# A decoder trunk's first stage: norm gains packed with the first tile of x, key weights in tiles of their own, first transfers in another order, first squares on Pool

## The chip, the cores and the metric

The kernel runs on one core of one Trainium2 chip. The core has TensorE (PE in the rows; PEld is its weight load), VectorE (DVE), ScalarE (ACT), GpSimd (POOL) and SyncE (SP), which here issues every transfer. They run side by side, each in the order of its own instructions, and wait for each other by semaphores. The metric is the device time of one execution in microseconds (us), the median of several runs.

## What is computed

Two layers of a decoder trunk over 576 tokens: 512 of a prompt and 64 of eight decode streams (8 tokens each, with 256 tokens in a paged cache). The model width is 1024.

```python
def decoder_layer(x, p_i, pos, ret_s0, past, topk, g_norm, w_in, q_gain, k_gain,
                  w_o_ret, w_o_att, w_out, w_ple_gate, w_ple_proj):
    h = rmsnorm(x, g_norm)
    rq, rk, rv, rz, aq, ak, av, az, iq, ik, iw, gr, ga = in_projection(h, w_in, pos, q_gain, k_gain)
    o_r, s_new = retention(rq, rk, rv, ret_s0)
...
    u_r = jnp.einsum('bte,ed->btd', o_r * jax.nn.silu(rz), w_o_ret)
...
    u_a = jnp.einsum('bte,ed->btd', o_a * jax.nn.silu(az), w_o_att)
    m = jax.nn.sigmoid(gr) * u_r + jax.nn.sigmoid(ga) * u_a
    x = x + jnp.einsum('btd,de->bte', m, w_out)
    gate = jax.nn.sigmoid(jnp.einsum('btd,de->bte', x, w_ple_gate))
    x = x + gate * jnp.einsum('btp,pd->btd', p_i, w_ple_proj)
    return x, ak, av, ik, s_new
```

Here `rmsnorm` divides x by the root of the mean of its squares over the 1024 channels and multiplies by a gain per channel, and `o_a` is an attention over keys that an indexer selects (top 128 of the prompt, top 66 of a decode stream). What the change touches is the norm of x and the projection to the indexer's key, the attention's key and its value (`ik`, `ak`, `av`: 64 + 128 + 128 = 320 columns).

## The kernel before

**Layout.** x lies with channels on the 128 partitions: eight tiles (k = 0 to 7) of 128 channels by 576 tokens. To keep precision, each operand of a product is split in a high part and a low rest, and a product is three matmuls: high by high, low by high, high by low. `put_x` makes them of a tile of x: ACT writes `xh` (x by the gain, rounded), DVE writes `xl` (x by the gain, less `xh`), and ACT copies the last 64 columns of `xl` behind `xh` (the "tail", used for the decode tokens). A weight tile `wst` becomes `whi` (ACT) and `wlo` (DVE, `wst` less `whi`) in `convert`.

**The norm's divisor** isn't applied to x. `put_x` also squares each tile of x (ACT, into `ssq`, shown as `rot`, or into slots of `misc`), and DVE adds the squares up tile by tile. When all eight are in, `stats` has PE sum over the channels (ten matmuls `tr<-ones,rot`), DVE and POOL make the reciprocal root `rcol`, and the results of the projections are scaled by it afterwards.

**The first stage** is `proj_kx`: for each k and each of five groups of tokens it multiplies `xh`, `xl` by the key weights of that k, into five banks (oT, acc, tq, pm, pm). That is 14 matmuls of 320 columns for each k, 112 in all; the last two k are done together, bank by bank. The key weights come in five parts (`KX_PARTS`: k 0, k 1, k 2 and 3, k 4 and 5, k 6 and 7), of 160 or 320 KB, through the same two `wst` and three `whi`/`wlo` slots as every other weight. Then the ten matmuls of `stats` follow, then the indexer's query projection (`iq`, 260 columns, weights in three parts), then the other projections. Layer 1 runs the same `proj_kx` at the end of layer 0.

**The order of the work** is made by the recorder `Streams` when the program is built: each generator yields operations, the recorder keeps a clock for every engine from its own table of durations, and takes next the operation that could start first (ties by priority). What it writes down is a fixed order on each engine; on the chip the semaphores alone decide when each starts. All operations are recorded in one helper, so that nearly all rows have its line, L309.

Of the kernel before, what the change touches and what calls it, by code (L numbers as in the profile page):

```python
# [21 lines left out]
KT = D // 128  # L22
NP = 512
NS = 64
T = NP + NS
TH = T // 2
TX = T + NS
DEPTH = 2
# [295 lines left out]
def tile_hybrid_decoder(ctx: ExitStack, tc: tile.TileContext, A, O):  # L324
    nc = tc.nc
    ctx.enter_context(tc.manual_schedule())
    K = Streams()
    V, S, PE, SP, G = (Engine(n, o) for n, o in (("DVE", nc.vector), ("ACT", nc.scalar), ("PE", nc.tensor),
                                                 ("SP", nc.sync), ("POOL", nc.gpsimd)))
# [36 lines left out]
    gn = cp.tile([128, DEPTH, KT], FT, name="gn")  # L366
# [5 lines left out]
    ssq = rot[:, 0:TX]  # L372
# [35 lines left out]
        K.set(paged)  # L408

    ready, paged = Event(), Event()  # L410
    second, third = Event(), Event()


    W = {}

    class Unit:
        def __init__(self, srcs):
            self.srcs, self.parts, self.ev = srcs, [], Event(len(srcs))
            self.evs = [Event() for _ in srcs]

    def plan(l):
        def b(key, n, per):
            src = A[key[0]][l] if len(key) == 1 else A[key[0]][l, key[1]]
            return [(src[:, k * n:min(KT, k + per) * n], (min(KT, k + per) - k) * n) for k in range(0, KT, per)]

        def a(i):
            return [(A["wa"][l, i], 1024)]

        for st in PLAN:
            name, i = st[0], st[1:]  # L430
            if name == "kx":
                srcs = [(A["wk"][l][:, a * 320:z * 320], (z - a) * 320) for a, z in KX_PARTS]
            elif name == "iq":
                srcs = b(("wq",), 260, 3)
            elif name in ("rv", "aq"):
                srcs = b(("wb", i[0] + (0 if name == "rv" else 2)), 256, 4)
            elif name in A_UNITS:
                srcs = a(A_UNITS[name] + i[0])
            elif name == "wo":
                srcs = [(A["wo"][l, i[0]], 1024)]  # L440
            elif name == "pp":
                srcs = [(A["wpp"][l, i[0]], 1024)]
            else:
                continue
            u = Unit(srcs)
            W[(l,) + st] = u
            yield u

    stage_ev = {}

    def load_weights(units):
        for n, (u, src, size) in enumerate(units):
            if n == 1:
                yield second
            if n == 3:
                K.set(third)
            t = yield Get(WST)
            yield SP.dma_start(t[:, :size], src)
            K.spawn(convert(u, t, size, stage_ev[n], stage_ev[n + 1]), PRIO["convert"])

    def convert(u, t, size, prev, done):
        yield prev
        hi = yield Get(WHI)
        lo = yield Get(WLO)
        yield S.activation(hi[:, :size], t[:, :size], AF.Copy)
        yield V.tensor_tensor(lo[:, :size], t[:, :size], hi[:, :size].bitcast(FT), OP.subtract)
        K.put(WST, t)
        K.set(u.evs[len(u.parts)])
        u.parts.append((hi, lo))
        K.set(u.ev)  # L470
        K.set(done)
# [48 lines left out]
    def proj_kx(u, xh, xl, evs):  # L520
        banks = []
        for name in ("oT", "acc", "tq", "pm", "pm"):
            banks.append((yield Get(BANK[name])))
        for i, (k0, k1) in enumerate(KX_PARTS):
            yield u.evs[i]
            if k1 < KT:
                order = [(k, j) for k in range(k0, k1) for j in range(5)]
            else:
                order = [(k, j) for j in range(5) for k in range(k0, k1)]
            for k, j in order:  # L530
                yield evs[k]
                hi, lo = (w[:, (k - k0) * 320:(k - k0 + 1) * 320] for w in u.parts[i])
                if j < 4:
                    c = slice(j * 128, (j + 1) * 128)
                    terms = ((xh[:, k, c], hi), (xl[:, k, c], hi), (xh[:, k, c], lo))
                else:
                    terms = ((xh[:, k, NP:TX], hi), (xh[:, k, NP:TX], lo))
                for n, (x, w) in enumerate(terms):
                    yield PE.matmul(banks[j][:, :320], x, w, start=k == 0 and n == 0,
                                    stop=k == KT - 1 and n == len(terms) - 1)  # L540
            K.put(WHI, u.parts[i][0])
            K.put(WLO, u.parts[i][1])
        return banks

    def split(hi, lo, x):
# [11 lines left out]
        yield G.tensor_tensor(dst, m[:n, :w], mh[:n, :w], OP.pow)  # L557
        K.put(RSM, m)

    def put_x(x, k, l, xh, xl, zs, first):  # L560
        yield S.activation(xh[:, k, :T], x, AF.Copy, scale=gn[:, l, k:k + 1])
        yield V.scalar_tensor_tensor(xl[:, k, :], x, gn[:, l, k:k + 1], xh[:, k, :T].bitcast(FT),
                                     op0=OP.mult, op1=OP.subtract)
        yield S.activation(xh[:, k, T:TX], xl[:, k, NP:T].bitcast(FT), AF.Copy)
        if k == 0:
            yield S.activation(ssq[:, :T], x, AF.Square)
            K.set(first)
        else:
            yield first
            sq = yield Get(zs)  # L570
            yield S.activation(sq, x, AF.Square)
            yield V.tensor_tensor(ssq[:, :T], ssq[:, :T], sq, OP.add)
            K.put(zs, sq)

# [3 lines left out]
    def layer(l, xh, xl, kxb):  # L578
# [818 lines left out]
        pl = lb.tile([128, 2, T], FR, name="pl")  # L1397
        pst = lb.tile([128, 2, T], FT, name="pst")

        def load_p():  # L1400
            yield SP.dma_start(pst, A["pT"][l])
            yield from split(ph, pl, pst)
# [76 lines left out]
        def ple2(d, th, ev):  # L1479
            yield ev  # L1480
            if last:
                K.put(ZS, th)
            else:
                yield e_pp[d]
                yield V.scalar_tensor_tensor(th, th, 1.0, pp[:, d], op0=OP.add, op1=OP.mult)
                yield V.scalar_tensor_tensor(xa[:, d], th, 0.5, xa[:, d], op0=OP.mult, op1=OP.add)
                K.put(ZS, th)
                yield from put_x(xa[:, d], d, l + 1, nh, nl, ZS, e_sq)
                K.set(e_n[d])
                yield SP.dma_start(xd[:, d, :], xa[:, d])  # L1490
            K.set(e_e)

        for d in range(KT):
# [11 lines left out]
    def main():  # L1505
        xh = xp.tile([128, KT, TX], FR, name="xh")
        xl = xp.tile([128, KT, T], FR, name="xl")
        K.spawn(setup(), 0)
        units = [(u, s, n) for l in range(DEPTH) for u in plan(l) for s, n in u.srcs]
        for n in range(len(units) + 1):  # L1510
            stage_ev[n] = Event(0 if n == 0 else 1)
        K.spawn(load_weights(units), PRIO["load"])
        evs = [Event() for _ in range(KT)]
        e_sq = Event()
        zs = zslots(0, 4)
        stc = tc.tile_pool(name="st", bufs=1, reuse_waits="tile")
        st = stc.__enter__()

        def load(k):
            x = st.tile([128, T], FT, name=f"x{k}")  # L1520
            if k > 3:
                yield third
            yield SP.dma_start(x, A["xT"][:, k, :])
            if k == 0:
                yield SP.dma_start(gn, A["norm_gain"])
                K.set(second)
            yield from put_x(x, k, 0, xh, xl, zs, e_sq)
            K.set(evs[k])

        for k in range(KT):  # L1530
            K.spawn(load(k), 2 if k else 0)
        K.spawn(setup2(), 3)
        kxb = yield from proj_kx(W[0, "kx"], xh, xl, evs)
        stc.__exit__(None, None, None)
        for l in range(DEPTH):
            xh, xl, kxb = yield from layer(l, xh, xl, kxb)
# [2 lines left out]
    K.go()  # L1539


KX_PARTS = ((0, 1), (1, 2), (2, 4), (4, 6), (6, 8))
BANKS = {"pm": 3, "tq": 1, "ta": 1, "oT": 1, "tr": 1, "acc": 1}
A_UNITS = {"az": 0, "rq": 4, "rk": 8, "rz": 12, "gr": 16, "ga": 24, "wout": 32, "wpg": 40}
# [19 lines left out]
def _prepare(x_prompt, x_sample, cache_k, cache_v, cache_idx_k, state_ret, page_table, p_prompt, p_sample,  # L1564
# [3 lines left out]
    def chan(a):  # L1568
        a = np.asarray(a)
        return a.reshape(a.shape[:-1] + (a.shape[-1] // 128, 128))  # L1570

    def tok(ap, as_):
        return np.concatenate([np.asarray(ap).reshape(NP, -1), np.asarray(as_).reshape(NS, -1)], 0)
# [1 line left out]
    d = {}  # L1575
    d["consts"], d["rot"] = _const_array()
    d["page_table"] = c(np.asarray(page_table).reshape(1, 16))
    d["norm_gain"] = c(chan(norm_gain).transpose(2, 0, 1))
    d["qk_gain"] = c(np.stack([np.asarray(q_norm_gain), np.asarray(k_norm_gain)], 1).reshape(-1))
    d["xT"] = c(chan(tok(x_prompt, x_sample)).transpose(2, 1, 0))  # L1580
    d["pT"] = c(np.stack([chan(tok(p_prompt[i], p_sample[i])).transpose(2, 1, 0) for i in range(DEPTH)]))
    w_in = np.asarray(w_in)
    offs = np.cumsum([0, 512, 512, 512, 512, 512, 128, 128, 512, 256, 64, 4, 1024, 1024])
# [60 lines left out]
```

## Time and profile before

| what | value |
|---|---|
| time, median of 3 runs | 1097.97 us (1097.46 to 1100.9) |
| the profiled execution's own time | 1100.1 us |
| its span, from the first to the last instruction | 1098.2 us |
| PE busy | 98% of the span |
| DVE busy | 69% |
| ACT busy | 48% |
| POOL busy | 6% |
| granted TensorE clock, mean | 0.997 |

The profile is of one execution. A busy PE need not be PE at its peak, since matmuls overlap; the time from one matmul's start to the next one's tells more. "Idle" before an instruction is the idle time of its engine, with what ended it.

### The profile page before, as it was taken

Reading aid. Unit: us, or ns where it says so; the run is one execution under the profiler, and the core shown is the slowest. Engines: PE = TensorE matmul, PEld = TensorE weight load, DVE = VectorE, ACT = ScalarE, POOL = GpSimd, SP = SyncE. Lnnn points to the kernel's source line nnn. Section 1 sums busy time; section 2 is a strip of 40 time slices with the busy share of each in tenths; the row PEclk is TensorE's granted clock in tenths of the full one; section 3 lists DMA queues with packets and bytes.
Section 4 is the critical chain, followed back from the end, with each engine's and each line's share of the span. In section 5 each row is a group of like instructions: output and inputs, shape, how many; then the busy total and the mean of one; then the engine's idle time right before and its main releaser. Section 6 shows DMA issues by size and latency. Waiting matters only on the chain.

```text
span 1098.2 us, 21521 instructions
## 1 busy us (share of the span) xinstructions
PE 1074.9 (98%) x8330; PEld 1048.6 (95%) x8330; DVE 759.6 (69%) x1963; ACT 527.4 (48%) x1112; POOL 68.6 (6%) x110
## 2 busy tenths in 40 slices
PE   7999999999999999999999999999999999999998
PEld 7989999989999999999999998999899999999998
DVE  6799999985455576543658999999854556655343
ACT  6743355676455442335446433656654555222421
POOL 0200012111000000000011001121101000000000
PEclk9999999999999999999999999999999999999999
DMA  6531222223333265533344322223232324554231
GB/s 204 162 118 69 88 80 96 76 83 110 113 103 108 103 198 158 184 93 104 99 124 133 108 71 74 81 99 106 91 121 91 121 90 144 184 184 136 82 115 49
DMA packets 53112, 124.85 MB, mean 114 GB/s; under 512 B 7443, under 2 KB 19603, under 8 KB 53011
## 3 DMA queue, kind: packets, MB, share of 16 engines
q1 hardware_dynamic: 53010, 123.49, 34.7%
q8 instruction: 65, 1.06, 0.4%
q14 instruction: 37, 0.30, 0.1%
HBM read 103.12 MB, written 20.35 MB: 112 GB/s over the span
## 4 chain that ended last, share of the span: by engine, by line
PE 68%; DVE 24%; issue 3%; DMA 1%; ACT 1%; SPq 1%; POOL 0%; DVEq 0%; POOLq 0%; ACTq 0%
PE pm L309 57%; DVE xl L309 6%; DVE sm L309 4%; DVE wlo L309 3%; PE tq L309 3%; PE oT L309 3%; DVE misc L309 2%; PE ta L309 2%; PE acc L309 2%; DVE silz L309 2%; PE tr L309 1%; DVE iqs L309 1%; DVE qs L309 1%; DVE tb L309 1%; DVE t2k L309 1%
## 5 line engine op out<-in xcount | busy, mean ns | idle before, releaser
L309 PE MATMUL pm<-xh,whi 128*128 128x288 f32 x1536 | 458.1, 298 | 0.0
L309 PE MATMUL pm<-xh,wlo 128*128 128x288 f32 x1536 | 457.5, 298 | 0.0
L309 PE MATMUL pm<-xl,whi 128*128 128x288 f32 x1536 | 457.2, 298 | 0.0
L309 PEld LDWEIGHTS pm<-xh,whi 128*128 128x128 f32 x1536 | 290.1, 189 | 1.2
L309 PEld LDWEIGHTS pm<-xl,whi 128*128 128x128 f32 x1536 | 290.2, 189 | 1.1 <-issue 0.2
L309 PEld LDWEIGHTS pm<-xh,wlo 128*128 128x128 f32 x1536 | 289.8, 189 | 0.9
L309 ACT ACTIVATE whi<-wst 128x1024 fp32r<-128x1024 f32 (+4 forms) x148 | 149.9, 1016 | 202.3 <-PE pm L309 135.0
L309 DVE TENSOR_TENSOR wlo<-wst,whi 128x1024 fp32r<-128x1024 f32 (+4 forms) x148 | 174.1, 1178 | 78.1 <-ACT whi L309 77.7
L309 PE MATMUL pm<-wlo,xh 128*128 128x256 f32 (+2 forms) x416 | 115.8, 287 | 1.7 <-DVE wlo L309 1.7
L309 PE MATMUL pm<-whi,xh 128*128 128x256 f32 (+2 forms) x416 | 117.0, 288 | 0.0
L309 PE MATMUL pm<-whi,xl 128*128 128x256 f32 (+2 forms) x320 | 91.6, 286 | 0.0
L309 ACT ACTIVATE t2k<-t2k,sm 128x256 f32<-128x256 f32 (+3 forms) x110 | 63.1, 579 | 43.7 <-DVE sm L309 42.2
L309 PEld LDWEIGHTS pm<-wlo,xh 128*128 128x128 f32 x416 | 78.7, 189 | 2.5 <-DVE wlo L309 2.3
L309 PEld LDWEIGHTS pm<-whi,xh 128*128 128x128 f32 x416 | 78.8, 189 | 1.9 <-issue 1.6
L309 PE MATMUL pm<-oh,whi 128*128 128x288 f32 x240 | 70.9, 296 | 0.0
L309 PE MATMUL pm<-oh,wlo 128*128 128x288 f32 x240 | 70.9, 295 | 0.0
L309 PE MATMUL pm<-ol,whi 128*128 128x288 f32 x240 | 70.8, 295 | 0.0
L309 PEld LDWEIGHTS pm<-whi,xl 128*128 128x128 f32 x320 | 60.5, 189 | 0.1
L309 DVE TENSOR_TENSOR misc<-pm,R 128x288 f32<-128x288 f32 x64 | 29.1, 455 | 42.1 <-PE pm L309 41.2
L309 DVE MAX8 sm<-xl 128x8 f32<-128x384 f32 (+2 forms) x96 | 52.2, 550 | 1.0
L309 DVE MATCH_REPLACE8 xl<-sm,xl 128x256 f32<-128x256 f32 (+2 forms) x96 | 51.7, 540 | 0.0
L309 DVE TENSOR_TENSOR ptl<-ta,pth 128x512 fp32r<-128x512 f32 (+1 forms) x48 | 28.6, 597 | 28.0 <-ACT pth L309 27.9
(261 smaller groups left out, 1723.7 us busy)
## 6 DMA issues: line engine op xcount, KB each, us to landing
wst<-in_wa SPq DMA_DIRECT2D x96, 512.0 KB, 3.5
wst<-in_wb SPq DMA_DIRECT2D x16, 512.0 KB, 4.0
wst<-in_wo SPq DMA_DIRECT2D x16, 512.0 KB, 3.9
zgr<-misc SPq DMA_DIRECT2D x16, 288.0 KB, 2.0
zga<-misc SPq DMA_DIRECT2D x16, 288.0 KB, 2.1
misc<-zgr SPq DMA_DIRECT2D x16, 288.0 KB, 2.8
misc<-zga SPq DMA_DIRECT2D x16, 288.0 KB, 4.6
s<-in_ckv SPq DMA_DIRECT2D x32, 128.0 KB, 2.4
```

The lines of the kernel that those rows point to most:

```text
L309: op.fn(*op.a, **op.k)
```

## The change

Five things. (1) The gains of both layers (16 columns) lie in memory behind the first tile of x, as `x0`, and come with it in one transfer; POOL copies them to `gn`, and the first `put_x` takes its gain from the tile itself. (2) The key weights of layer 0 get tiles of their own, raw (`kxs`) and split (`kx`, two of them, high and low), and those of layer 1 get two split tiles; so they no longer pass through the shared slots (layer 1's still come through `wst`). (3) x and the key weights are issued by one stream in the order in which they are used; the indexer's weights come next, and the constants after those. (4) The high part of the first key weights is made by DVE (`tensor_copy`), not by ACT. (5) `put_x` no longer squares; a new `square` follows it, on POOL in layer 0 (`tensor_tensor` of x by x) and on ACT, as before, in layer 1.

```diff
     def load_weights(units):
         for n, (u, src, size) in enumerate(units):
-            if n == 1:
-                yield second
-            if n == 3:
-                K.set(third)
-            t = yield Get(WST)
+            own = None
+            if u.kx is not None:
+                yield go_kx[n] if u.kx == 0 else e_kxw
+                a, z = (k * 320 for k in KX_PARTS[u.srcs.index((src, size))])
+                own = [w[:, a:z] for w in kxw[u.kx]]
+            if u.kx == 0:
+                t = kxw["raw"][:, a:z]
+            else:
+                t = yield Get(WST)
             yield SP.dma_start(t[:, :size], src)
-            K.spawn(convert(u, t, size, stage_ev[n], stage_ev[n + 1]), PRIO["convert"])
...
+    def kx_tiles(pool, l):
+        return [pool.tile([128, KT * 320], FR, name=f"kx{i}{l}") for i in range(2)]
+
+    def convert(u, t, size, prev, done, own, first):
         yield prev
-        hi = yield Get(WHI)
-        lo = yield Get(WLO)
-        yield S.activation(hi[:, :size], t[:, :size], AF.Copy)
+        if own is None:
+            hi = yield Get(WHI)
+            lo = yield Get(WLO)
+        else:
+            hi, lo = own
+        if first:
+            yield V.tensor_copy(hi[:, :size], t[:, :size])
+        else:
+            yield S.activation(hi[:, :size], t[:, :size], AF.Copy)
         yield V.tensor_tensor(lo[:, :size], t[:, :size], hi[:, :size].bitcast(FT), OP.subtract)
...
-            K.put(WHI, u.parts[i][0])
-            K.put(WLO, u.parts[i][1])
         return banks
...
+    def square(x, k, zs, first, eng):
+        def sq2(dst):
+            if eng is S:
+                return S.activation(dst, x, AF.Square)
+            return eng.tensor_tensor(dst, x, x, OP.mult)
+
         if k == 0:
-            yield S.activation(ssq[:, :T], x, AF.Square)
+            yield sq2(ssq[:, :T])
             K.set(first)
         else:
             yield first
             sq = yield Get(zs)
-            yield S.activation(sq, x, AF.Square)
+            yield sq2(sq)
             yield V.tensor_tensor(ssq[:, :T], ssq[:, :T], sq, OP.add)
             K.put(zs, sq)
...
+        if l + 1 < DEPTH:
+            kxw[l + 1] = kx_tiles(lb, l + 1)
+            K.set(e_kxw)
...
-                yield from put_x(xa[:, d], d, l + 1, nh, nl, ZS, e_sq)
+                yield from put_x(xa[:, d], d, gn[:, l + 1, d:d + 1], nh, nl)
                 K.set(e_n[d])
                 yield SP.dma_start(xd[:, d, :], xa[:, d])
+                yield from square(xa[:, d], d, ZS, e_sq, S)
...
-        def load(k):
-            x = st.tile([128, T], FT, name=f"x{k}")
-            if k > 3:
-                yield third
-            yield SP.dma_start(x, A["xT"][:, k, :])
+        def take(k, x):
+            gain = gn[:, 0, k:k + 1]
             if k == 0:
-                yield SP.dma_start(gn, A["norm_gain"])
-                K.set(second)
-            yield from put_x(x, k, 0, xh, xl, zs, e_sq)
+                yield G.tensor_copy(flat(gn), x[:, T:])
+                x, gain = x[:, :T], x[:, T:T + 1]
+            yield from put_x(x, k, gain, xh, xl)
             K.set(evs[k])
-
-        for k in range(KT):
-            K.spawn(load(k), 2 if k else 0)
+            yield from square(x, k, zs, e_sq, G)
+
+        def load():
+            for k in range(KT):
+                x = st.tile([128, T if k else T + DEPTH * KT], FT, name=f"x{k}")
+                yield SP.dma_start(x, A["xT"][:, k, :] if k else A["x0"])
+                K.spawn(take(k, x), 0)
+                if k in STEPS:
+                    K.set(go_kx[STEPS.index(k)])
+            K.set(third)
...
+STEPS = (0, 1, 3, 5, 7)
```

What this makes of POOL's program at its start (x_139 is the tile with the first x and the gains, x_142 to x_165 the other seven tiles; `rot` and `misc` take the squares):

```order
L309 COPY gn<-x_139 128x16
L309 ISA
L309 TENSOR_TENSOR rot<-x_139 128x576
L309 TENSOR_TENSOR misc<-x_142 128x576
L309 TENSOR_TENSOR misc<-x_147 128x576
L309 TENSOR_TENSOR misc<-x_150 128x576
L309 TENSOR_TENSOR misc<-x_152 128x576
L309 TENSOR_TENSOR misc<-x_157 128x576
L309 TENSOR_TENSOR misc<-x_160 128x576
L309 TENSOR_TENSOR misc<-x_165 128x576
L309 MEMSET xl 64x64
```

Before, five memsets stood here, then the ISA row (the program's request for a library of POOL's), then the `rcol` of `stats`; the eight squares are new, and the five memsets and `rcol` follow them.

DVE's program in the first stage, before, from the first tile of x on (`rot<-rot,misc` adds a square to the sum):

```order
L309 SCALAR_TENSOR_TENSOR xl<-x_138,gn,xh 128x576
L309 SCALAR_TENSOR_TENSOR xl<-x_139,gn,xh 128x576
L309 TENSOR_TENSOR rot<-rot,misc 128x576 x2
L309 TENSOR_TENSOR wlo_126<-wst_119,whi_123 128x640
L309 TENSOR_TENSOR rot<-rot,misc 128x576
L309 TENSOR_TENSOR wlo_124<-wst_120,whi_121 128x640
L309 SCALAR_TENSOR_TENSOR xl<-x_140,gn,xh 128x576
```

And the same stretch of DVE's program after the change, with the copy at its start:

```order
L309 CAST kx_136<-kxs 128x320
L309 SCALAR_TENSOR_TENSOR xl<-x_139,xh 128x576
L309 TENSOR_TENSOR kx_137<-kxs,kx_136 128x320
L309 SCALAR_TENSOR_TENSOR xl<-x_142,gn,xh 128x576
L309 TENSOR_TENSOR kx_137<-kxs,kx_136 128x320
L309 SCALAR_TENSOR_TENSOR xl<-x_147,gn,xh 128x576
L309 TENSOR_TENSOR rot<-rot,misc 128x576
L309 SCALAR_TENSOR_TENSOR xl<-x_150,gn,xh 128x576
L309 TENSOR_TENSOR rot<-rot,misc 128x576
L309 TENSOR_TENSOR kx_137<-kxs,kx_136 128x640
L309 TENSOR_TENSOR rot<-rot,misc 128x576
```

The same eight `xl`, five low parts and seven sums stand there as before, with the one copy added; each sum now comes behind a square of POOL's, and the sums stand further forward among the `xl`.

## Rows read from the trace of the kernel before

**Rows 1.** The page: busy time of each engine over the span.

```profile
PE 1074.9 (98%) x8330; PEld 1048.6 (95%) x8330; DVE 759.6 (69%) x1963; ACT 527.4 (48%) x1112; POOL 68.6 (6%) x110
```

**Rows 2.** Timeline of PE: start, duration, instruction, idle before it and its releaser.

```profile
5.10 0.64 PE L309 MATMUL oT<-whi,xh 128*128 128x320 f32 x1 [5.10 <-ACT whi L309]
...
6.70 0.47 PE L309 MATMUL acc<-whi,xl 128*128 128x320 f32 x1
6.97 0.47 PE L309 MATMUL acc<-wlo,xh 128*128 128x320 f32 x1
...
12.48 0.41 PE L309 MATMUL oT<-wlo,xh 128*128 128x320 f32 x1 [0.47 <-DVE wlo L309]
...
20.80 0.41 PE L309 MATMUL oT<-wlo,xh 128*128 128x320 f32 x1
...
24.43 0.31 PE L309 MATMUL pm<-whi,xh 128*128 128x320 f32 x1
24.57 0.31 PE L309 MATMUL pm<-wlo,xh 128*128 128x320 f32 x1
24.72 1.17 PE L309 MATMUL tr<-ones,rot 128*128 128x1 f32 x10
...
29.30 0.65 PE L309 MATMUL tr<-cst,rcol 128*128 128x128 f32 x4 [0.21 <-POOL rcol L309]
...
38.86 0.28 PE L309 MATMUL pm<-whi,xl 128*128 128x256 f32 x1
39.93 0.39 PE L309 MATMUL pm<-wlo,xh 128*128 128x256 f32 x1 [0.79 <-DVE wlo L309]
```

**Rows 3.** Timeline of DVE, first stage; xN is a run of N instructions.

```profile
4.73 0.82 DVE L309 SCALAR_TENSOR_TENSOR xl<-x,gn,xh 128x576 fp32r<-128x576 f32 x1 [3.81 <-ACT xh L309]
5.46 0.48 DVE L309 TENSOR_TENSOR wlo<-wst,whi 128x320 fp32r<-128x320 f32 x1
6.50 0.49 DVE L309 TENSOR_TENSOR wlo<-wst,whi 128x320 fp32r<-128x320 f32 x1 [0.55 <-ACT whi L309]
7.88 2.28 DVE L309 SCALAR_TENSOR_TENSOR xl<-x,gn,xh 128x576 fp32r<-128x576 f32 x3 [0.89 <-ACT xh L309]
10.08 1.61 DVE L309 TENSOR_TENSOR rot<-rot,misc 128x576 f32<-128x576 f32 x2
...
16.66 3.34 DVE L309 TENSOR_TENSOR rot<-rot,misc 128x576 f32<-128x576 f32 x4
19.92 1.70 DVE L309 TENSOR_TENSOR wlo<-wst,whi 128x640 fp32r<-128x640 f32 x2
```

**Rows 4.** Timeline of ACT: the first high part of x, and one of the eight squares.

```profile
3.92 0.78 ACT L309 ACTIVATE xh<-x,gn 128x576 fp32r<-128x576 f32 x1 [1.68 <-DMA gn<-in_norm_gain]
...
9.23 0.67 ACT L309 ACTIVATE misc<-x 128x576 f32<-128x576 f32 x1
```

**Rows 5.** Timeline of SP: the second transfer, start and time of its issue.

```profile
1.19 0.41 SPq L309 DMA_DIRECT2D gn<-in_norm_gain  x1
```

**Rows 6.** Timelines of POOL and DVE around two products that POOL makes.

```profile
351.33 0.74 POOL L309 TENSOR_TENSOR silz<-t2k,silz 128x256 f32<-128x256 f32 x1 [24.57 <-DVE t2k L309]
...
351.40 1.74 DVE L309 TENSOR_TENSOR wlo<-wst,whi 128x1024 fp32r<-128x1024 f32 x1 [0.16 <-ACT whi L309]
...
833.60 1.77 POOL L309 TENSOR_TENSOR silz<-t2k,silz 128x256 f32<-128x256 f32 x1 [8.38 <-DVE t2k L309]
...
833.55 1.23 DVE L309 TENSOR_TENSOR wlo<-wst,whi 128x1024 fp32r<-128x1024 f32 x1
```

**Rows 7.** Groups of DVE by form: count, busy us, mean ns, idle before.

```profile
L309 DVE TENSOR_TENSOR wlo<-wst,whi 128x1024 fp32r<-128x1024 f32 x132 | 162.2, 1229 | 62.8 <-ACT whi L309 62.5
```

**Rows 8.** Timeline of POOL, start of the program.

```profile
1.71 0.10 POOL L309 MEMSET xl<- 64x4 f32 x1
28.07 1.17 POOL L309 TENSOR_TENSOR rcol<-rsm,mh 128x5 f32<-128x5 f32 x1 [26.26 <-DVE rsm L309]
```

**Rows 9.** The chain that ended last, one of its longest pieces.

```profile
393.79 159.21 PE pm L309 x1200
```

More of the change, by code (lines that the diff above doesn't have):

```diff
@@ L410, in tile_hybrid_decoder, with __init__ @@
     ready, paged = Event(), Event()
-    second, third = Event(), Event()
+    third, e_kxw = Event(), Event()
+    kxw = {}
+    go_kx = [Event() for _ in KX_PARTS]
     W = {}
     class Unit:
-        def __init__(self, srcs):
-            self.srcs, self.parts, self.ev = srcs, [], Event(len(srcs))
+        def __init__(self, srcs, kx=None):
+            self.srcs, self.parts, self.ev, self.kx = srcs, [], Event(len(srcs)), kx
             self.evs = [Event() for _ in srcs]
@@ L444, in plan @@
                 continue
-            u = Unit(srcs)
+            u = Unit(srcs, l if name == "kx" else None)
             W[(l,) + st] = u
@@ L452, in load_weights @@
         for n, (u, src, size) in enumerate(units):
-            if n == 1:
-                yield second
-            if n == 3:
-                K.set(third)
-            t = yield Get(WST)
-            yield SP.dma_start(t[:, :size], src)
-            K.spawn(convert(u, t, size, stage_ev[n], stage_ev[n + 1]), PRIO["convert"])
-    def convert(u, t, size, prev, done):
-        yield prev
-        hi = yield Get(WHI)
-        lo = yield Get(WLO)
-        yield S.activation(hi[:, :size], t[:, :size], AF.Copy)
+            own = None
[7 more added lines that the diff above has]
+                t = yield Get(WST)
+            yield SP.dma_start(t[:, :size], src)
+            K.spawn(convert(u, t, size, stage_ev[n], stage_ev[n + 1], own, n == 0), PRIO["convert"])
+    kxs = None
+    def kx_tiles(pool, l):
+        return [pool.tile([128, KT * 320], FR, name=f"kx{i}{l}") for i in range(2)]
+    def convert(u, t, size, prev, done, own, first):
+        yield prev
+        if own is None:
[7 more added lines that the diff above has]
+            yield S.activation(hi[:, :size], t[:, :size], AF.Copy)
         yield V.tensor_tensor(lo[:, :size], t[:, :size], hi[:, :size].bitcast(FT), OP.subtract)
-        K.put(WST, t)
+        if u.kx != 0:
+            K.put(WST, t)
         K.set(u.evs[len(u.parts)])
@@ L558, in rsqrt, with put_x @@
         K.put(RSM, m)
[L560 to L563, printed above, removed]
+    def put_x(x, k, gain, xh, xl):
+        yield S.activation(xh[:, k, :T], x, AF.Copy, scale=gain)
+        yield V.scalar_tensor_tensor(xl[:, k, :], x, gain, xh[:, k, :T].bitcast(FT), op0=OP.mult, op1=OP.subtract)
         yield S.activation(xh[:, k, T:TX], xl[:, k, NP:T].bitcast(FT), AF.Copy)
+    def square(x, k, zs, first, eng):
[3 more added lines that the diff above has]
+            return eng.tensor_tensor(dst, x, x, OP.mult)
         if k == 0:
-            yield S.activation(ssq[:, :T], x, AF.Square)
+            yield sq2(ssq[:, :T])
             K.set(first)
@@ L1517, in main @@
         st = stc.__enter__()
-        def load(k):
-            x = st.tile([128, T], FT, name=f"x{k}")
-            if k > 3:
-                yield third
-            yield SP.dma_start(x, A["xT"][:, k, :])
+        def take(k, x):
+            gain = gn[:, 0, k:k + 1]
             if k == 0:
-                yield SP.dma_start(gn, A["norm_gain"])
-                K.set(second)
-            yield from put_x(x, k, 0, xh, xl, zs, e_sq)
+                yield G.tensor_copy(flat(gn), x[:, T:])
+                x, gain = x[:, :T], x[:, T:T + 1]
+            yield from put_x(x, k, gain, xh, xl)
             K.set(evs[k])
-        for k in range(KT):
-            K.spawn(load(k), 2 if k else 0)
+            yield from square(x, k, zs, e_sq, G)
[7 more added lines that the diff above has]
+            K.set(third)
+        kxw[0] = kx_tiles(st, 0)
+        kxw["raw"] = st.tile([128, KT * 320], FT, name="kxs")
+        K.spawn(load(), PRIO["load"])
         K.spawn(setup2(), 3)
@@ L1577, in _prepare @@
     d["page_table"] = c(np.asarray(page_table).reshape(1, 16))
-    d["norm_gain"] = c(chan(norm_gain).transpose(2, 0, 1))
     d["qk_gain"] = c(np.stack([np.asarray(q_norm_gain), np.asarray(k_norm_gain)], 1).reshape(-1))
     d["xT"] = c(chan(tok(x_prompt, x_sample)).transpose(2, 1, 0))
+    d["x0"] = c(np.concatenate([d["xT"][:, 0], chan(norm_gain).transpose(2, 0, 1).reshape(128, -1)], 1))
     d["pT"] = c(np.stack([chan(tok(p_prompt[i], p_sample[i])).transpose(2, 1, 0) for i in range(DEPTH)]))
```

## The prediction

> **What bounds the kernel now.** I read the page first: PE is busy for 98% of the span [rows 1], so the end moves by what is added to PE's waits or taken from them. A piece of the chain that ended last shows how tight the middle is: 1200 matmuls in 159 us without another engine in between [rows 9]. So the question is the first 40 us, and there I read PE's timeline, then DVE's. PE begins at 5.10, its early matmuls start 0.27 us apart, later ones 0.146 apart, and the key projection's last matmul is followed by the sums of squares at 24.72. Up to there PE waits visibly once, for a low part made by DVE (0.47 idle before 12.48); the low part of k 6 and 7 comes just in time at 20.80 [rows 2]. DVE's timeline says why: from 7.88 on it has no idle time, up to 19.92 + 1.70 = 21.6; before that it idles 0.55 and 0.89 [rows 3]. The last low part of the keys is the first of the two in the row at 19.92, so it ends at about 20.74, and PE's matmul at 20.80 follows it by 0.06. In this stage DVE paces PE as much as PE paces itself. What makes a DVE instruction later here makes the kernel longer.
>
> **The change, part by part.**
>
> *Gains with x.* ACT's first `xh` waits for the gains' transfer until 3.92 [rows 4], and its issue holds SP from 1.19 for 0.41 us [rows 5]. Without it the weights behind it can come up to 0.45 earlier. ACT itself gains less, since x still has to land: between 0 and 0.45; I take 0.15, so `xh` starts at 3.77 and ends at 4.55.
>
> *Order of transfers, key weights in own memory.* The waits for shared slots go. The only visible stall they could cure in this stage is the one at 12.48 (0.47), and its low part also stood behind sums in DVE's queue. For layer 1 there is nothing to win: PE has no wait in the long run of [rows 9], which lies in front of layer 1's key projection, and I count 0. The indexer's weights now come ahead of the constants and are split before `stats`; from 24.72 to the transposes at 29.30 [rows 2] I take off the 0.5 that the walk below gives (bounds 0, and 0.7 with the 0.21 that PE idles there). The constants come later, but are needed only behind `stats`.
>
> *First high part on DVE.* One copy of 320 columns, at most the 0.48 of the low part of the same size [rows 3]. ACT no longer makes it behind the first `xh`, but the first `xl` now stands behind the copy on DVE, and it isn't late by more than the copy: between 0.48 later and 0.5 earlier for PE's first matmul, which the walk below settles.
>
> *Squares from ACT to POOL.* ACT loses eight instructions of 0.67 [rows 4]; ACT isn't what DVE waits for after 7.88, so by itself that gives only the 1.4 of DVE's early idle time. POOL gains eight products of 576 columns, and nothing like them stands in this stage before: POOL rests from 1.8 to 28.07 [rows 8]. The nearest rows are POOL's products of 256 columns later on [rows 6]. Alone, one takes 0.74. But look at DVE beside it: a low part of 1024 columns, which takes 1.23 on average [rows 7], began 0.07 after POOL's product at 351.33 and took 1.74. It was held until 0.07 + 1.74 - 1.23 = 0.58 after POOL's start. The other way round, at 833.60, POOL began 0.05 behind such a low part and took 1.77 instead of 0.74: it waited until DVE had read its operands. So a POOL product that reads two operands from the on-chip memory and a DVE instruction that reads two there exclude each other. All of DVE's `xl`, low parts and sums are of that kind.
>
> The Trainium skill states this too (SBUF — State Buffer, "Who interferes with whom"): a DVE instruction with two inputs in SBUF and a GpSimd instruction that reads SBUF exclude each other, and whoever comes first keeps the port for the whole instruction. By "the whole instruction" the hold would be 0.74, where the rows show 0.58; grown with the columns that is 1.66 for a square, and the walk below ends 9.7 - 7.0 = 2.7 us later with it; the measurement decides.
>
> How long does a square hold DVE? By columns, 0.58 x 576/256 = 1.31, call it 1.33. If 0.1 of it were fixed, the length of POOL's smallest memset [rows 8], it is 1.2. The ends: 0.59 if the hold didn't grow at all, and 0.74 x 2.25 = 1.66 if the whole of POOL's instruction held and grew. I take 1.33, since a loop over columns is the plain reading.
>
> The sum. Eight holds are 8 x 1.33 = 10.6 us, put into a stage in which DVE had 1.4 us free [rows 3]. Off this go the 1.4; some 0.5 of the first hold, which begins at about 3.85, before DVE's first weights are there; and 8 x 0.15 for the part of a waiting DVE instruction that isn't reading columns (1.23 for 1024 and 0.48 for 320 columns are 1.07 ns a column and 0.14 fixed [rows 3, 7]). That leaves 10.6 - 1.4 - 0.5 - 1.2 = 7.5. A walk through the new orders of DVE, POOL, ACT and PE with these durations, whoever asks first going first, gives 7.0: first matmul at 5.5, if the copy, too, waits for the first square; low part of k 4 and 5 at 23.8; low part of k 6 and 7 at 27.5 instead of 20.74; sums of squares at 31.7 instead of 24.72. Who goes first matters little, because each sum waits for its square in DVE's order: if DVE always won, it would stand still at the sums instead. The same walk gives +1.3 at a hold of 0.59, +6.0 at 1.2, +9.7 at 1.66, and 0 at about 0.45.
>
> Behind that, 0.5 off as above, and something of the 0.79 that PE idles for a low part before 39.93 [rows 2]: 0 to 0.79, I take 0.4, because the order there stays much the same. POOL's five memsets now stand behind the squares, and `rcol` behind both; the squares end at about 21.6 in the walk and `rcol` is wanted ten us later, so the memsets cost nothing, and without that cover at most the 1.8 us at which the last of them ends now [rows 8]. From there PE is full and carries the shift to the end. In sum 7.0 - 0.5 - 0.4 = 6.1, say **6 us longer**. The profiled execution took 1100.1 around a span of 1098.2, which would become 1106; the median of the runs is 2.1 below that execution, so I forecast 1097.97 + 6 = 1104.0.
>
> **The rivals.**
>
> *The squares don't hold DVE (ends on the other side).* For it: POOL's products of [rows 6] read two different tiles, a square reads one tile twice, and POOL idles before. Against it: both orders of arrival in [rows 6]. The walk without holds ends the key projection 1.1 earlier, since no low part is late; with 0.5 and 0.4 that is 2.0 faster, 1096.0 (1095 to 1096.5). It decides from a hold of some 0.5 us downward.
>
> *The hold is short, or partly hidden.* Somewhere between 0.59 and 0.95 a square: 0.4 to 3.3 us slower, 1100. For it: the row shows one width only, so that the growth with columns is my reading.
>
> *POOL starts late.* The ISA row stands directly ahead of the first square. Before, whatever it takes lay in the 26.26 idle us ahead of `rcol` [rows 8], which bounds it between 0 and 26. In the walk a delay of 3 us costs 0.8 more, and 6 us cost 3.0 more, since the first sum stands ahead of `xl` of k 3 and waits for the second square: 1107.
>
> The Trainium skill (GPSIMD Engine Reference, "Instruction dispatch") gives about 6 us, invisible in a profile, for the first call into a freshly loaded library; no row here shows it, and by it the sum would be 1107.
>
> *PE stays slow.* With a pause in front of nearly every k, PE might keep the early spacing: 112 x 0.27 = 30 us from 5.5 on, some 4 more than the walk, 1108. For it: only that the early spacing is there; against it: the pause at 12.48 brought none.
>
> **How the numbers follow.** Chances: the forecast's own case 0.46 (own range 1101.5 to 1107); squares that don't hold DVE 0.20; short or hidden hold 0.17; late POOL 0.12; slow PE 0.05. About 0.3% (3.3 us) is what a measurement of this kernel can tell from no change. Slower by more: 0.46 + 0.12 + 0.05 = 0.63. Within: 0.17, and 0.13 of the first rival's 0.20, since 2.0 is below 3.3. Faster by more: the remaining 0.07, if more of the later waits went than I take off. The range goes from 1096.0 (half of the first rival's case lies below, 0.10) to 1108.2 (0.06 above).
>
> **What would show it.** In the changed profile: DVE instructions of 576 columns that take about 2.1 us instead of 0.8 in the first 22 us, and squares of POOL stretched to 2 us where DVE came first; the low part of k 6 and 7 near 27 us; the ten matmuls on `rot` near 31.7. If DVE's durations there stay at 0.75 to 0.82 and the ten matmuls stand near 23.6, the hold was wrong. If POOL's first square starts several us after its copy of the gains, POOL was late. If matmuls stay 0.27 apart after 12 us, PE was slow. What would make it wrong without these is a shift made good later: then PE's rows from 45 us on would stand less than 5 us behind those of before.

## The result and the profile after

The changed kernel takes 1105.8 us (median of 4 runs, 1105.5 to 1106.8) beside 1098.36 for the kernel before (median of 4): ratio 1.0066, 95% interval 1.0047 to 1.0084. It is slower by 7.4 us, where 6 were forecast (1104.0). The span of the profiled execution grew from 1098.2 to 1105.0. The size is right, but it is not made of what the forecast was made of, so the rows below go through the span in order.

The page's busy line answers to [rows 1]:

```profile
PE 1074.0 (97%) x8330; PEld 1048.5 (95%) x8330; DVE 766.2 (69%) x1964; ACT 521.3 (47%) x1103; POOL 80.2 (7%) x119
```

POOL's timeline at the start (it rested here before, [rows 8]):

```profile
3.68 0.20 POOL L309 COPY gn<-x 128x16 f32<-128x16 f32 x1 [3.23 <-DMA x<-in_x]
3.91 1.15 POOL L309 TENSOR_TENSOR rot<-x 128x576 f32<-128x576 f32 x1
...
14.99 1.66 POOL L309 TENSOR_TENSOR misc<-x 128x576 f32<-128x576 f32 x1 [0.69 <-DVE rot L309]
```

The first square starts 0.03 us behind the copy's end: POOL was not late. A square that meets nobody takes 1.15 us, and 1.66 where DVE came first.

DVE's timeline, at the start (answers to [rows 3]) and near 588 us:

```profile
4.13 1.11 DVE L309 CAST kx<-kxs 128x320 fp32r<-128x320 f32 x1 [3.21 <-DMA kxs<-in_wk]
5.16 0.80 DVE L309 SCALAR_TENSOR_TENSOR xl<-x,xh 128x576 fp32r<-128x576 f32 x1
...
9.97 1.70 DVE L309 TENSOR_TENSOR rot<-rot,misc 128x576 f32<-128x576 f32 x1
11.59 1.70 DVE L309 SCALAR_TENSOR_TENSOR xl<-x,gn,xh 128x576 fp32r<-128x576 f32 x1
13.21 1.70 DVE L309 TENSOR_TENSOR rot<-rot,misc 128x576 f32<-128x576 f32 x1
14.83 0.81 DVE L309 TENSOR_TENSOR kx<-kxs,kx 128x640 fp32r<-128x640 f32 x1
...
19.54 0.75 DVE L309 TENSOR_TENSOR rot<-rot,misc 128x576 f32<-128x576 f32 x1
...
588.06 0.76 DVE L309 TENSOR_TENSOR rot<-rot,R 128x576 f32<-128x576 f32 x1 [3.54 <-DMA rot<-in_rot]
588.74 1.22 DVE L309 TENSOR_TENSOR wlo<-wst,whi 128x1024 fp32r<-128x1024 f32 x1
```

Sums and `xl` that meet a square take 1.70 instead of 0.75 or 0.80: each is held 0.9 to 0.95 us. Five instructions are held that long (those that start at 9.97, 11.59, 13.21, 15.57 and 17.92); the copy and two early `xl` (6.89, 9.05) meet only a part of a square, 0.8, 0.3 and 0.2 us. The eight squares thus hold DVE for 5.9 us in all. PE's timeline shows what that does:

```profile
5.38 0.61 PE L309 MATMUL oT<-kx,xh 128*128 128x320 f32 x1 [5.38 <-DVE kx L309]
...
15.70 0.42 PE L309 MATMUL oT<-kx,xh 128*128 128x320 f32 x1 [2.67 <-DVE kx L309]
15.95 0.31 PE L309 MATMUL acc<-kx,xh 128*128 128x320 f32 x1
16.10 0.31 PE L309 MATMUL acc<-kx,xl 128*128 128x320 f32 x1
...
21.07 0.41 PE L309 MATMUL oT<-kx,xh 128*128 128x320 f32 x1 [1.01 <-DVE kx L309]
...
29.09 1.17 PE L309 MATMUL tr<-ones,rot 128*128 128x1 f32 x10
...
53.43 0.39 PE L309 MATMUL tq<-kdh,iqs 128*128 128x256 f32 x1 [1.75 <-DVE iqs L309]
...
62.10 0.63 PE L309 MATMUL ta<-cst,t2k 128*128 128x128 f32 x4 [0.71 <-DVE t2k L309]
...
63.95 0.39 PE L309 MATMUL pm<-wlo,xh 128*128 128x256 f32 x1 [0.63 <-DVE wlo L309]
...
585.20 0.28 PE L309 MATMUL pm<-whi,xl 128*128 128x256 f32 x1
590.01 0.58 PE L309 MATMUL pm<-wlo,xh 128*128 128x256 f32 x1 [4.53 <-DVE wlo L309]
```

Where [rows 2] had one wait of 0.47, two of 2.67 and 1.01 for low parts stand now, and the ten matmuls on `rot` come at 29.09 instead of 24.72. Of these 4.4 us, 0.3 are the later first matmul, 2.2 and 1.2 what the two waits are longer than before, and 0.7 come from PE's early spacing of 0.27, which lasts until 11.4 instead of 9.6. Then there are waits that no step of the forecast had: three in layer 0, and one of 4.53 us in layer 1. The same matmul in both traces gives the shift:

| matmul (of its kind, the n-th) | before | after | shift |
|---|---|---|---|
| `tr<-ones,rot`, 1st | 24.72 | 29.09 | +4.37 |
| `pm<-whi,xl`, 54th | 47.90 | 50.82 | +2.92 |
| `pm<-whi,xl`, 74th | 60.47 | 65.94 | +5.47 |
| `pm<-xh,whi`, 230th | 221.89 | 227.19 | +5.30 |
| `pm<-xh,whi`, 273rd | 261.77 | 262.96 | +1.19 |
| `tr<-cst,rcol`, 10th | 575.63 | 578.54 | +2.91 |
| `pm<-xh,whi`, 842nd | 648.98 | 657.94 | +8.96 |
| `pm<-xh,whi`, 1470th | 1067.04 | 1073.91 | +6.87 |

In the changed kernel the split key weights are named `kx`; its `pm<-kx,xl` are counted as `pm<-whi,xl` here. So 2.9 us arrive at layer 1, the wait there adds 6.0, and 2.1 of the sum come back by some 930 us. Why does layer 1 wait? SP's timeline of the changed kernel there:

```profile
572.38 11.48 SPq L393 DMA_DIRECT2D s<-in_cik  x16
583.96 0.53 SPq L309 DMA_DIRECT2D rot<-in_rot  x1
```

The tables' transfer stands behind sixteen page gathers. That isn't new, as SP's timeline of the kernel before shows (5 and 11 gathers, and the transfer 2.7 us earlier, about as much as the changed kernel is late here):

```profile
567.68 3.95 SPq L393 DMA_DIRECT2D s<-in_cik  x5
...
572.46 7.09 SPq L393 DMA_DIRECT2D s<-in_cik  x11
...
581.22 0.38 SPq L309 DMA_DIRECT2D rot<-in_rot  x1
```

What is new is that the chain of waits goes through it:

```profile
583.96 4.07 DMA rot<-in_rot
...
588.06 0.06 DVE rot L309
...
588.74 1.23 DVE wlo L309
```

The low part that PE wants needs nothing of that transfer; it only stands behind `rot<-rot,R` in DVE's order. The kernel before had both low parts ahead of the tables there, as its DVE timeline shows:

```profile
581.74 1.22 DVE L309 TENSOR_TENSOR wlo<-wst,whi 128x1024 fp32r<-128x1024 f32 x1
...
583.01 1.22 DVE L309 TENSOR_TENSOR wlo<-wst,whi 128x1024 fp32r<-128x1024 f32 x1
...
585.74 1.41 DVE L309 TENSOR_TENSOR rot<-rot,R 128x576 f32<-128x576 f32 x2
```

Windows of the changed kernel (columns: window, PE, PEld, DVE, ACT, POOL, granted clock, DMA share, GB/s) show a second price of the wait:

```profile
584.00:588.00 4.00, 1.48 (x13) 1.28 (x11) 0.52 (x5) 2.96 (x8) 0.00 (x0) 1.00 0.70 198
588.00:590.00 2.00, 0.00 (x0) 0.00 (x0) 1.94 (x3) 0.00 (x0) 0.52 (x1) 0.56 0.05 14
590.00:592.00 2.00, 1.99 (x9) 1.99 (x10) 2.00 (x7) 0.00 (x0) 0.00 (x0) 0.50 0.42 78
592.00:594.00 2.00, 2.00 (x11) 2.00 (x10) 1.33 (x7) 0.00 (x0) 0.00 (x0) 0.50 0.97 293
594.00:596.00 2.00, 2.00 (x15) 2.00 (x14) 0.00 (x0) 0.76 (x3) 0.39 (x2) 0.73 0.78 248
596.00:600.00 4.00, 4.00 (x36) 4.00 (x35) 2.85 (x8) 3.11 (x10) 0.24 (x2) 1.00 0.24 51
```

While PE waits, its clock falls to 0.50 (1.2 instead of 2.4 GHz) and stays there until some 5 us after it begins again: 35 matmuls in 590 to 596, where at the last row's 36 in 4 us there would be 54; the 19 that are missing are some 2 us. With the 4.1 us by which the wait exceeds the one that the kernel before has at this place (4.7 against 0.6, from one matmul's start to the next, less the usual spacing), this makes about the 6.0.

The kernel before has such a stretch in its profiled execution too, which the forecast did not look for. Its windows:

```profile
242.00:244.00 2.00, 1.63 (x5) 1.44 (x6) 1.19 (x4) 0.83 (x2) 0.00 (x0) 0.50 0.47 125
244.00:246.00 2.00, 2.00 (x11) 2.00 (x10) 0.92 (x2) 0.73 (x2) 0.00 (x0) 0.50 0.34 137
246.00:248.00 2.00, 2.00 (x9) 1.77 (x9) 1.34 (x2) 0.59 (x3) 0.00 (x0) 0.50 0.00 0
```

Six us at half speed are 3 us, and the changed kernel stays at 1.00 there: that is most of the 4.1 that the table gives back between 227 and 263 us. Beside an execution of the kernel before without this stretch, the shift would be some 4.2 at 263 us and 5.9 ahead of layer 1.

### The profile page after: what moved, and what is told of

It reads as the page before. It is cut to its first block, busy times and chain, and to the rows that moved or that the text cites. A ratio compares the mean times of both kernels' runs of the same rounds, so it can differ in the third digit from the quotient of the medians.

```text
span 1105.0 us, 21497 instructions
## 1 busy us (share of the span) xinstructions
PE 1074.0 (97%) x8330; PEld 1048.5 (95%) x8330; DVE 766.2 (69%) x1964; ACT 521.3 (47%) x1103; POOL 80.2 (7%) x119
## 4 chain that ended last, share of the span: by engine, by line
PE 73%; DVE 19%; issue 4%; DMA 2%; ACT 1%; POOL 1%; SPq 1%; DVEq 0%; POOLq 0%; ACTq 0%
PE pm L309 61%; DVE xl L309 5%; PE tq L309 3%; DVE sm L309 3%; PE oT L309 3%; DVE misc L309 2%; PE acc L309 2%; DVE wlo L309 2%; PE ta L309 2%; PE tr L309 2%; DVE silz L309 1%; DVE qs L309 1%; DMA rot<-in_rot 1%; DVE iqs L309 1%; DVE t2k L309 1%
## 5 line engine op out<-in xcount | busy, mean ns | idle before, releaser
L309 ACT ACTIVATE whi<-wst 128x1024 fp32r<-128x1024 f32 (+1 forms) x138 | 144.0, 1046 | 192.7 <-PE pm L309 126.2
L309 DVE TENSOR_TENSOR wlo<-wst,whi 128x1024 fp32r<-128x1024 f32 (+1 forms) x138 | 168.2, 1219 | 65.9 <-ACT whi L309 65.7
L309 PE MATMUL pm<-wlo,xh 128*128 128x256 f32 (+1 forms) x384 | 107.6, 288 | 5.6 <-DVE wlo L309 5.6
L309 PE MATMUL pm<-whi,xh 128*128 128x256 f32 (+1 forms) x384 | 107.2, 287 | 0.0
L309 PE MATMUL pm<-whi,xl 128*128 128x256 f32 (+1 forms) x304 | 87.6, 288 | 0.0
L309 PEld LDWEIGHTS pm<-wlo,xh 128*128 128x128 f32 x384 | 73.6, 192 | 7.1 <-DVE wlo L309 6.2
L309 PEld LDWEIGHTS pm<-whi,xh 128*128 128x128 f32 x384 | 73.6, 192 | 0.5 <-issue 0.4
L309 DVE MAX8 sm<-xl 128x8 f32<-128x512 f32 (+2 forms) x96 | 52.2, 550 | 0.9
L309 DVE MATCH_REPLACE8 xl<-sm,xl 128x384 f32<-128x384 f32 (+2 forms) x96 | 51.8, 540 | 0.0
L309 POOL TENSOR_TENSOR sm<-rsm,mh 128x4 f32<-128x4 f32 (+3 forms) x30 | 31.6, 1053 | 277.6 <-DVE rsm L309 276.9
```

The lines of the kernel that those rows point to most:

```text
L309: op.fn(*op.a, **op.k)
```

## The experiments

Two theories, each with a rival: **A**, the squares on POOL hold DVE, and that is the cost of the first stage; **B**, layer 1's cost is the order that the recorder wrote there, independent of the squares.

**1. Squares on ACT.** In the changed kernel:

```
-            yield from square(x, k, zs, e_sq, G)
+            yield from square(x, k, zs, e_sq, S)
```

> The changed kernel, but layer 0's squares of x stand on ACT again, as in the kernel before. Theory A (a square on POOL holds DVE, and that is the cost of the first stage): DVE's sums and low parts of the first 25 us take 0.75 to 0.82 us instead of 1.70, and the ten matmuls on rot stand at 23.6 to 24.7 instead of 29.09. Theory B (the other cost is a written order: in layer 1 the tables' product stands ahead of a low part of the rv weights on DVE and waits for its own transfer): the wait of some 4.7 us near 585 us stays, since this order is unchanged, and the kernel stands 2.5 to 4.5 us below the changed one, 1101 to 1103, above the kernel before. Rival to B (the wait of layer 1 is only the shift of the first stage, come out in another place): the wait goes with the shift, and the kernel stands at or below the one before, 1096 to 1098.

1102.71 us, ratio to the kernel before 1.0043 (1.003 to 1.0057). The sums and low parts take 0.75 to 0.82 again, and the copy 0.33. PE's timeline:

```profile
25.09 0.95 PE L309 MATMUL tr<-ones,rot 128*128 128x1 f32 x8
...
586.86 0.58 PE L309 MATMUL pm<-wlo,xh 128*128 128x256 f32 x1 [4.78 <-DVE wlo L309]
```

The first stage gets 4.0 us back, a little less than expected (25.09, not 23.6 to 24.7), and 3.1 of them are left at the end. That is 1105.8 less 1102.71; these two stood beside different runs of the kernel before (medians 1098.36 and 1097.71), and with each set against its own it is 2.4. DVE's order is the same in both kernels up to the sum at 15.57, behind the low part that PE waits 2.67 us for. Here PE waits 0.76 and 0.36 us in that place, so that the rest is made by the holds and not by another order. Layer 1's wait stays, with the clock at 0.50 behind it: A and B hold, and B's rival, that this wait is the shift come out elsewhere, falls.

**2. Only the squares on POOL**, in the kernel before:

```
-            yield S.activation(sq, x, AF.Square)
+            yield G.tensor_tensor(sq, x, x, OP.mult)
```

(and likewise for the first, in layer 0 alone).

> The kernel before with one edit: layer 0's squares of x are POOL's products instead of ACT's activations. Theory A: DVE instructions of 576 columns that meet a square take 1.7 us instead of 0.8, the ten matmuls on rot come 3 to 5 us behind 24.72, and no wait of 4 us appears near 585 us, since the order of layer 1 is the old one; of the 3 to 5 us some 2 to 4 are left at the end, 1100 to 1102. Rival (the squares cost nothing by themselves, the first stage is late for the new order of its transfers): the ten matmuls stay within 0.5 us of 24.72, 1098.

1099.89 us, ratio 1.0016 (1.0006 to 1.0025): slower, as A has it, by less than the 1100 to 1102 expected. The first stage is 5.5 us later, where 3 to 5 were expected:

```profile
16.48 0.63 PE L309 MATMUL oT<-wlo,xh 128*128 128x320 f32 x1 [4.17 <-DVE wlo L309]
...
30.20 1.17 PE L309 MATMUL tr<-ones,rot 128*128 128x1 f32 x10
```

Behind the 4.17 us the clock is at 0.52 from 18 to 20 us. Layer 1 has no long wait. Of the 5.5, some 2 are left at the end (1099.89 less 1097.71): the rest is made good on the way.

**3. Tables behind the weights**, in the changed kernel:

```
             yield SP.dma_start(rot, A["rot"])
+            yield W[l, "rv", 0].ev
             yield V.tensor_tensor(cosr, cosr, R, OP.mult)
```

> The changed kernel, but the tables' product with the rotation's signs is not written before the first of the rv weights' parts is converted, so that in layer 1 DVE has both low parts ahead of it; layer 0's order stays as it is, and so do POOL's squares. Theory B: the wait near 585 us falls from 4.7 to below 1, and the kernel ends 3 to 5 us below the changed one, 1101 to 1103. Rival (layer 1's wait comes from the key weights' own memory or from transfers that are late by themselves): the wait only changes its name, the low part then waits for its own weights, and the time stays within 1 us of 1105.8.

1102.06 us, ratio 1.0039 (1.0028 to 1.005). DVE's timeline has the low parts first:

```profile
583.86 1.21 DVE L309 TENSOR_TENSOR wlo<-wst,whi 128x1024 fp32r<-128x1024 f32 x1
...
585.13 1.21 DVE L309 TENSOR_TENSOR wlo<-wst,whi 128x1024 fp32r<-128x1024 f32 x1
...
587.24 0.74 DVE L309 TENSOR_TENSOR rot<-rot,R 128x576 f32<-128x576 f32 x1
```

PE's wait there is 0.34, its clock stays at 1.00, and 3.7 us are gone (3.1, each against its own runs of the kernel before). The weights were there in time, and layer 1's key memory, which is untouched here, doesn't cost by itself: B.

**4. Both edits**, 1 and 3.

> Both edits on the changed kernel: layer 0's squares on ACT, and in layer 1 both low parts of the rv weights ahead of the tables' product on DVE. If theories A and B hold and are independent, their gains add: 6 to 9 us below the changed kernel, 1097 to 1100, about the kernel before or a little below. Rival (one cause, seen in two places): the sum is no better than the better of the two edits alone, 1101 to 1103.

1098.8 us, ratio 1.0007 (0.9998 to 1.0017). The gains add within the scatter: 3.1 and 3.7 alone, 7.0 together; each against its own runs of the kernel before, 2.4 and 3.1 alone, 6.4 together.

**5. Layer 1's key weights through the shared slots**, in the changed kernel:

```
-            u = Unit(srcs, l if name == "kx" else None)
+            u = Unit(srcs, l if name == "kx" and l == 0 else None)
...
```

(and with that the two split tiles of layer 1 are not made, and its slots are given back as before).

> The changed kernel, but layer 1's key weights go through the shared slots again, as in the kernel before; POOL's squares stay. With that DVE's order in layer 1 is the old one by itself: one low part of the rv weights ahead of the two table products. Theory B (the order is what waits near 585 us): no wait above 1 us there, no stretch of the lower clock behind it, and 3 to 5 us below the changed kernel, 1101 to 1103, as in the run that only moved the tables' product. Rival (the shift of the first stage or the transfer itself makes that wait): the wait of 4 us and more stays, 1105 to 1106.

1101.37 us, ratio 1.0032 (1.002 to 1.0044). The recorder then writes both low parts ahead of the tables by itself (at 583.39 and 584.66, the tables' products at 587.39), and PE waits 0.44 there. So the key memory costs by the order that it makes the recorder write.

**6. Squares in halves**, to see how a hold grows:

```
...
+                for a in (0, TH):
+                    yield eng.tensor_tensor(dst[:, a:a + TH], x[:, a:a + TH], x[:, a:a + TH], OP.mult)
```

> The changed kernel, but each of POOL's eight squares is two products of 288 columns, so that the same columns are read by twice as many instructions. It asks how a product's hold of DVE grows with its size. If the hold has a fixed part (0.58 us at 256 columns and some 0.93 at 576 make 0.3 fixed and 1.1 ns a column), a half holds 0.62, the two of a square 1.25, and the first stage ends 1 to 2.5 us later than at 29.09, with the end 0.5 to 2.5 us later, 1106 to 1108. If the hold goes by columns alone, the two halves hold what the whole did, and the ten matmuls on rot stay within 0.7 us of 29.09, with the end within 1 us of 1105.8.

1105.73 us. Both expectations of the stage's end fail: the ten matmuls begin at 27.85, 1.2 us earlier. The recorder wrote another order here, too: the low part of k 2 and 3 stands one sum further forward on DVE and ends at 13.05 instead of 15.64. The holds are plain, though. In the view of the tile `misc` (durations in ns, min/median/max) POOL's halves take, and in DVE's timeline a sum beside them takes:

```profile
L309 POOL TENSOR_TENSOR misc<-x x14: 679/1177/1257, 5.8 to 20.4; 128x288 f32<-128x288 f32 x14
```

```profile
16.39 1.22 DVE L309 TENSOR_TENSOR rot<-rot,misc 128x576 f32<-128x576 f32 x1
```

A half holds 1.22 - 0.75 = 0.47, a whole square 0.95: by columns, 1.65 ns each, with no fixed part that shows.

**7. Two tiles.** The same products, but of x and its high part:

```
-            return eng.tensor_tensor(dst, x, x, OP.mult)
+            return eng.tensor_tensor(dst, x, xh[:, k, :T].bitcast(FT), OP.mult)
```

> The changed kernel, but each of POOL's eight products reads two tiles, x and its high part, in place of x twice (so the norms are of another product, and the output is not the reference's). It asks why a square of 576 columns holds DVE for 0.95 us, 1.6 ns a column, where the forecast took 2.3 ns from a product of 256 columns in two tiles. If reading two tiles makes the difference, a lone product of 576 columns takes about 1.5 us instead of 1.15, DVE instructions that meet one take 2.0 to 2.1 us instead of 1.70, and the first stage ends 2 to 3 us later than at 29.09. If not, they stay 1.15 and 1.70.

1108.04 us in one run. The same two views:

```profile
L309 POOL TENSOR_TENSOR misc<-x,xh x7: 1419/1911/2054, 6.4 to 20.9; 128x576 f32<-128x576 f32 x7
```

```profile
15.61 1.97 DVE L309 TENSOR_TENSOR rot<-rot,misc 128x576 f32<-128x576 f32 x1
```

A lone product takes 1.42 instead of 1.15 and holds 1.97 - 0.75 = 1.22 instead of 0.95; both are near what was expected. The ten matmuls come at 34.13, 5.0 us later than in the changed kernel, where 2 to 3 were expected: PE waits 3.47 us for a low part before 23.58, and behind that its clock is at 0.50 from 24 to 28 us. So at one size it is reading two tiles that makes a product dearer, as far as this one pair of tiles shows.

**8. Tables early.** Experiment 4, and the tables ranked ahead of the gathers:

```
-PRIO = dict(convert=0, load=1, tables=6, indexer=7, indexer_s=3, attend=3, attend_s=5, ret_p=6, ret_s=4)
+PRIO = dict(convert=0, load=1, tables=2, indexer=7, indexer_s=3, attend=3, attend_s=5, ret_p=6, ret_s=4)
```

> The changed kernel with layer 0's squares on ACT and the rv weights ahead of the tables, as in the run of both edits, and one thing more: the tables rank ahead of the page gathers, so that SP issues their transfer behind the third gather instead of the seventeenth. Theory: DVE's table products in layer 0 no longer wait 3.1 us for their transfer, PE's wait of 1.65 us at 54.96 goes, and of it 1 to 2.5 us are left at the end: 1096 to 1098, 0 to 2 us below the kernel before. Rival (the waits of layer 0 are made good later anyway, by the slack that the changed kernel's shift of 5.5 us also lost half of there): within 0.7 us of the run of both edits, 1098.1 to 1099.5.

1104.67 us, ratio 1.0055 (1.0042 to 1.0069): a miss. The local gain came: PE's waits between 47 and 60 us are gone (one of 1.79 stands at 45.68), and until 220 us most of PE's rows are 0.2 to 2.3 us ahead of the kernel before. But the recorder wrote the end of layer 0 otherwise, and PE idles several times there. The windows:

```profile
252.00:254.00 2.00, 1.05 (x4) 0.69 (x4) 1.54 (x6) 2.00 (x7) 0.00 (x0) 0.58 0.63 215
254.00:258.00 4.00, 4.00 (x29) 3.20 (x29) 0.69 (x4) 0.90 (x3) 0.00 (x0) 0.50 0.02 4
258.00:262.00 4.00, 3.31 (x16) 2.95 (x15) 2.46 (x9) 0.70 (x2) 0.80 (x2) 0.50 0.00 0
```

Some nine us at about 0.50 cost some 4.5.

**9. Squares on ACT and layer 1 through the shared slots** (experiments 1 and 5 together).

> The changed kernel with layer 0's squares on ACT and layer 1's key weights in the shared slots, so that of the change there stay the packed gains, the order of the first transfers, the first high part on DVE, and layer 0's key weights in their own memory. If what the two single edits gave back adds (3.1 and 4.4 us of 1105.8), 1098.3, within 1 us of the kernel before; no wait above 1 us near 585 us and no lower clock there. If the parts that stay are worth something by themselves, as the first stage's 0.7 to 1.2 us ahead at 47 us in the run of both edits suggests, and layer 0's later waits (1.06 and 1.65 us there) do not appear here, 1096.5. Rival (the written order of layer 0 turns out otherwise again): another place loses 2 us or more, 1100 to 1104, as in the run with the tables early.

1098.09 us beside 1098.11, ratio 0.9999 (0.999 to 1.0008). What is left of the change here, the packed gains, the order of the first transfers, the copy on DVE and layer 0's own key memory, is worth nothing that can be measured, with an interval of about 1 us either way. In its profile PE is 1.65 us ahead of the kernel before at 48 us, and new waits (0.54 before 47.78, 1.55 before 56.18) use that up by 60 us. No version beat the kernel before.

## Why the prediction was right, and which of its steps were not

**Gains with x, first matmul: right.** ACT's first `xh` starts at 3.65 (3.77 forecast, 3.92 before [rows 4]), the first matmul at 5.38 (5.5): the copy is held by the first square, 1.11 us, where it takes 0.33 in experiment 1, in which the square is ACT's and the first matmul starts at 4.62.

**Squares hold DVE: right in kind, the size of one hold wrong.** The step was "by columns, 0.58 x 576/256 = 1.31, call it 1.33"; it measured 0.95. Growing it by columns was sound (experiment 6). What failed is the row that it grew from: the product of [rows 6] reads two tiles, a square one tile twice, and at the same 576 columns that is 1.22 against 0.95 (experiment 7). The prediction named this difference, but only as a reason why there might be no hold at all. Between the walk's own values, +1.3 at 0.59 and +6.0 at 1.2, a straight line gives +4.1 for 0.95; the stage measured +4.4, not +7.0, and the low part of k 6 and 7 ends at 24.55, not 27.5. The prediction gives the walk's ends and not its steps, so only these can be compared. The count was too large as well: the sum took eight whole holds, 10.6 us less 0.5, and five whole ones and three parts came, 5.9 us. Experiment 1 takes 4.0 of the 4.4 back, so the cause is shown.

The Trainium skill (SBUF — State Buffer, "Who interferes with whom") has whoever issues first keep the shared ports for the whole instruction. The exclusion is seen both ways; the hold is 0.2 us shorter than the lone product in all three widths and kinds (0.47 of 0.68, 0.95 of 1.15, 1.22 of 1.42), and the measurement decides.

**Rivals of the first stage.** No hold: falls. A short hold "between 0.59 and 0.95": its upper end is where the hold lies, but its 1100 isn't the time, because of layer 1. Late POOL: falls (0.03 us). By the Trainium skill (GPSIMD Engine Reference, "Instruction dispatch") a first call to freshly loaded code costs about 6 us that no profile shows; the rows here leave no room for it ahead of the first square, which begins right behind the library's request. Slow PE: falls in the main. The spacing is 0.15 again from 11.4 on, which is 1.8 us later than before, and costs 0.7 instead of the 4 that the rival has.

**Later waits, -0.5 and -0.4: right in kind.** The shift falls by 1.45 until 48 us, against 0.9: by 1.1 until 33 us, and by 0.3 at the low part that [rows 2] has at 39.93.

**Layer 1, "I count 0": wrong, and the largest miss.** PE had no wait in front of layer 1's key projection, as [rows 9] said, and none came. The cost came behind it, through the recorder: other memory means other ready times, so that another order is written. It put a table product ahead of the low part that PE waits for, while the tables' transfer stood behind its sixteen gathers as before: 4.1 us of wait and 2 us at the lower clock. Experiments 3 and 5 each take the wait away, 3.7 and 4.4 us, with POOL's squares in place. The order after the change was there to be read, and the forecast read it in the first stage alone.

**"From there PE is full and carries the shift to the end": only in part.** The shift goes 4.4, 2.9, 5.5, 1.2, 2.9, 9.0, 6.9. The sign that the prediction set against itself, rows less than 5 us behind from 45 us on, did show, at 2.9. Most of the fall to 1.2 belongs to the profiled execution of the kernel before, which loses 3 us at the lower clock there. By the runs' times, of the 4.0 us of experiment 1 some 2.4 to 3.1 are left at the end, and of the 5.5 of experiment 2 some 2.2. So the squares are worth some 2 to 3 us at the end, not 6.1. The forecast of 6 stands beside a measured 7.4 (6.9 in the profiled executions) because a term too large by 2.6 and a shift partly made good were replaced by a wait of which it knew nothing: the direction has its cause in the forecast, the size is luck. Layer 0 has new waits of its own (53.43 and 62.10 to 63.95, together +2.6 between the table's rows at 48 and 60 us). Between the same rows experiment 4 has +2.4 and experiment 9 +2.1, but experiments 5 and 8 have -0.4 and -0.7, so that they belong to no single edit; what causes them stays open.

## What to carry to other kernels

Where a planner writes the order, read the new order at every place where the critical engine waits, not only where the code was edited; look for an instruction that waits for a transfer of its own ahead of one that the critical engine needs. Before work goes to an idle engine, ask what it reads beside whom, and take the price from a row that reads the same operands. A wait of several us can cost TensorE its clock as well; in layer 1 this part was half as large as the wait, 2 us beside 4.1.

## What the runs showed that was not expected

The clock gave no fixed answer to the same wait. In the changed kernel PE idles 2.67 us before 15.70 and the clock stays at 1.00; in the profile of experiment 5 it idles 2.57 at the same place and the clock is at 0.50 from 16 to 22 us. The kernel before itself ran between 1096.3 us at a mean clock of 1.000 and 1100.2 at 0.996 in the 25 runs beside experiments 1 to 4, with one order of instructions. In all four runs of the changed kernel the mean was 0.996. A profile against a profile can thus carry some 3 us that belong to neither kernel.
